# Differential attention, second layer: squares, lambda and the last transpositions at other places, one low weight part per head on VectorE

## The chip, the cores and the metric

One core of a Trainium2 chip (trn2) runs the program. TensorE (PE) multiplies and transposes. VectorE (DVE), ScalarE (ACT) and GpSimd (POOL) work element by element. SyncE (SP) issues the DMAs. The metric is the device time of one execution in microseconds.

## The reference

The model has two layers over 512 latent tokens and 256 context tokens of width 1024. The first layer has windowed and dense attention and is not touched. The second is differential attention with eight heads, and only it matters here:

```
hx = rms(x, w) * (1 + scale) + shift              # x: 512 x 1024;  hc the same from ctx: 256 x 1024
q, k, v = split([hc; hx] @ w_in)                  # eight heads, two q and two k of 64 each, v of 128
q, k = rope(rms(q)), rope(rms(k))                 # only the latent tokens are rotated
lam = exp(sum(lq1*lk1)) - exp(sum(lq2*lk2)) + lam_init
a = softmax(q0 k0^T / 8) - lam * softmax(q1 k1^T / 8)
o = rms(a @ v, subln) * (1 - lam_init)
x = x + gate * (o @ w_out);  then a feed-forward layer
```

## The kernel before

All large products are made in two parts: an operand is split into a high part (rounded, a cast on ScalarE) and a low part (what is left, a subtraction on VectorE or GpSimd), and hi·hi, lo·hi and hi·lo are summed in PSUM. The tokens lie in six tiles of 128: 0 to 3 are latent, 4 and 5 context.

The program is written as Python that calls the engines. TensorE's order is the order of writing. For the other engines a scheduler in the framework takes, by its own estimates, the next instruction that is ready; `behind(name)` keeps an instruction from being issued before the last one that was noted under this name in `turn`, and `tc.high_priority` lifts one. So a piece that is written elsewhere, or on another engine, moves neighbours too.

The second layer's attention goes like this.

- **Last normalizations** (`last_norm0`, `norm_steps`). For the latent tiles 1 to 3, ScalarE squares a row block of x and sums it (`nss`), GpSimd forms the inverse root (`rs_n`) and scales x (`nh`), TensorE transposes `nh` (`npt`), VectorE and ScalarE apply scale and shift and split the result into `hT` high and low. This is written between the first head's products (`inps`): context tiles 4 and 5, then tile 0, then tiles 1 to 3 together.
- **Projection** (`Proj1.sums`, `finish`). Per head and tile TensorE sums 1024 x 384 (context 256) products, with weight units of 256 rows: `wir` is loaded by DMA, `wih` is its cast, `wil` the subtraction (`weight1`, line 377). A head has four units, u = 0 to 3. Then ScalarE copies `inps` to `qkv`, VectorE and GpSimd rotate and normalize, and the casts `qd` and `kd` with their low parts go out. With `hold` these last are kept back, and written behind the copy of the next tile. TensorE transposes them later (`qpt`, `kpt`, from the list `late`), and ScalarE copies them to `qt` and `kT`.
- **Attention** (`attend1`). Each step is one tile of one head, 32 in all. TensorE makes two score tiles (`sc`), VectorE their maxima (`mx`), ScalarE exponentials with sums (`e`), VectorE combines them with lambda (`rt`, `e`), TensorE transposes (`ppt`), ScalarE copies four and VectorE two of the six pieces (`PT`), TensorE multiplies with V (`av`), ScalarE scales and squares (`o`), GpSimd forms `rs_o`, VectorE scales by it. Projection of the next head is written in three parts between the stages (`step`).
- **Tail.** In the last steps no projection is left, and the output projection (`opt`, `ops`, class `OutProj`) is written between the stages instead. `part(0)` is its first term, `oproj.operand` the transposition of `o` and its split.

All of this shares PSUM: two banks for transpositions (`tr_tile`, in turn), two for sums (`acc_tile`), and two pairs for scores (`sc`), of which the pairs hold tiles 0 to 3 of the first head before the first scores.

The line

```
                new_head([weight1(h, u, wh, nc.vector if h == 1 and u == 3 else nc.gpsimd) for u in range(4)])
```

sets the engine of each `wil` of heads 1 to 7: all on GpSimd but one.

Of the kernel before, what the change touches and what calls it, by code (L numbers as in the profile page):

```python
# [11 lines left out]
F32 = mybir.dt.float32  # L12
# [51 lines left out]
def backbone(es: ExitStack, tc: tile.TileContext, x, c, ctx, c_ctx, mod_w, mod_b, norm_mix_w, norm_ffn_w,  # L64
# [91 lines left out]
    def rsqrt(ss, n, inv, tag):  # L156

        r = small.tile([P, n], F32, name="rs_" + tag, tag="rs_" + tag)
        nc.gpsimd.tensor_scalar(r, ss, inv, EPS, ALU.mult, ALU.add)
        nc.gpsimd.tensor_tensor(r, r, neghalf[:, :n], ALU.pow)  # L160
        return r
# [164 lines left out]
    def tile_T(j, t):  # L326
        return cols_T(j, t * P, (t + 1) * P)

    def norm_steps(t, xt, l, f, pool, tags=(("nh", 2), ("nhc", 2)), room=None, bank=tr_tile, to=None, pool_scale=False):

        i = 0 if t < NTX else 1
        h, hc = room or (pool.tile([P, KT, P], F32, name=name, tag=tag, bufs=n)
                         for name, (tag, n) in zip(("nh", "nhc"), tags))
        halves = hc if isinstance(hc, list) else [hc[:, 0:4], hc[:, 4:8]]
        ss = small.tile([P, 1], F32, name="nss", tag="nss")
        xt = xt.rearrange("p (k c) -> p k c", c=P)
        turn["square"] = nc.scalar.activation(h, xt, AF.Square, accum_out=ss)
        r = rsqrt(ss, 1, 1.0 / D, "n")  # L340
        if pool_scale:
            turn["pool_scale"] = nc.gpsimd.tensor_scalar(h, xt, r, 1.0, ALU.mult, ALU.mult)
        else:
            turn[f"scaled{t}"] = nc.scalar.activation(h, xt, AF.Copy, scale=r)
        yield
        for g in range(2):
            pt = bank("npt", [P, 4, P])
            for k in range(4):
                turn["npt"] = nc.tensor.transpose(pt[:, k, :], h[:, 4 * g + k, :], ident)  # L349
            ks = slice(4 * g, 4 * g + 4)  # L350
            for k in range(4):
                kk = 4 * g + k
                sc, sh = aff[l][:, f, kk, i:i + 1], modc[l][:, 3 * f, kk, i:i + 1]
                if g:
                    nc.scalar.activation(halves[g][:, k], pt[:, k, :], AF.Identity, bias=sh, scale=sc)
                else:
                    nc.vector.tensor_scalar(halves[g][:, k], pt[:, k, :], sc, sh, ALU.mult, ALU.add)
            hi, lo = (to(j, g) if to else tile_T(j, t)[:, ks] for j in range(2))
            turn["hi"] = nc.scalar.copy(hi, halves[g])
            (nc.gpsimd if g and not pool_scale else nc.vector).tensor_sub(lo, halves[g], f32(hi))  # L360
# [1160 lines left out]
    if True:  # L1521
# [50 lines left out]
        def early_weight(u):  # L1572
            def room(shape, name):
# [5 lines left out]
        hooks = {(1, 0): [open_ctx], (1, 3): [finish_norm(4)], (1, 5): [finish_norm(5)], (1, 7): [finish_norm(0)],  # L1579
                 (1, 8): [small_loads], (1, 10): [lambda: ws1.append(head_tables(wt.pool, od_qn[0], od_kn[0], 2, 2))]}  # L1580
        hooks |= {(1, 12 + 2 * u): [early_weight(u)] for u in range(4)}
        way_out0(xs, hidm, out0.pool, places, raws, mod_hook1, hooks, done0)
    singles.close()
    p_sc = Pool("p_sc1", space=PSUM)
# [1 line left out]
    mods1.close()  # L1586
    wp = Pool("mw1", "right")
    wh = (whi.pool, wlo.pool)
    lqk, tabs = ws1[:2]
    del ws1[:2]  # L1590
    fp.close()
    at = Pool("mix1")
# [9 lines left out]
    def halves():  # L1602
        for h in range(1, 8):
            with behind(*("exp0",) * (h == 2)):
                new_head([weight1(h, u, wh, nc.vector if h == 1 and u == 3 else nc.gpsimd) for u in range(4)])
            for t in CTX_FIRST:
                ps = acc_tile("inps", one=0)
                state[h].sums(t, ps, range(4))
                yield t
                state[h].sums(t, ps, range(4, KT))  # L1610
                late.append((count + 5, state[h].finish(t, ps, count < 5)))
                yield t

    todo = halves()
# [11 lines left out]
    def last_norm0(t):  # L1626
        h, hc = (raw_tile([P, KT, P], "nhc") if t == 2 and i else keep.tile([P, KT, P], F32, name="nh", tag="xo", bufs=6)
                 for i in range(2))
        with tc.high_priority(300):
            for _ in norm_steps(t, xs[t], 1, 0, None, room=(h, hc), pool_scale=True):  # L1630
                pass

    if True:
        new_head(ws1)
        first = state[0]
        banks = {t: acc_tile("inps") for t in CTX_FIRST[:2]}
        for t in (0, 2):
            two = p_sc.pool.tile([P, 2, 512], F32, name="inps", tag="sc", bufs=2)
            banks.update({t + a: two[:, a, :] for a in range(2)})

        def ready(t):
            late.append((0, first.finish(t, banks[t], 0 < t < NTX)))

        for t in CTX_FIRST[:2]:
            first.sums(t, banks[t], range(KT))
# [16 lines left out]
        for i in range(6):  # L1662
            step()
            if i:
                turned()
        nlam = neg_lambda(lqk, cp)
        with behind("load"):
            subln = at.pool.tile([P, P], F32, name="subln")
            nc.sync.dma_start(subln, dram_rows(od_subln[0]))
            nc.gpsimd.tensor_scalar(subln, subln, 1.0 - LAM_INIT, 1.0, ALU.mult, ALU.mult)  # L1670
        xs0, xs1 = xs, [None] * NTX
        gate_mem(1, 5, 1)
        o_t = [keep.tile([P, D], F32, name=f"o{t}", tag="xo", bufs=6) for t in range(NTX)]
        xs = xs1
        attend = {}
# [8 lines left out]
        def transposed(i):  # L1684
            next(attend[i])
# [59 lines left out]
               *((nc.gpsimd, 4) if len(ws) in (3, 4, 6) else (nc.vector, 1)))  # L1745

        scores(last - 1)
        oproj.operand(0, ((0, 4),), acc1)
        transposed(last - 2)
        part(0)  # L1750
        while late:
            turned(True)
        values(last - 2)
        wp.close()
        wt.close()
        whi.close()
# [5 lines left out]
        opa = Pool("opa", "right")  # L1762
        oproj.gates(opa.pool)
        wo1()
        scores(last)
        transposed(last - 1)
        part(1, 2)
        values(last - 1)
        wo1()
        scores(last + 1)  # L1770
        oproj.operand(0, ((4, 7),), acc1)
# [192 lines left out]
```

## Time and profile before

| what | value |
|---|---|
| timed runs | 1684.29, 1685.66, 1688.02 us (median 1685.66) |
| profiled execution | 1689.65 us, of which the span of its instructions is 1687.9 |
| mean granted clock of TensorE | 0.994 |
| TensorE busy | 1629.1 us (97% of the span) |
| VectorE, ScalarE, GpSimd busy | 1141.2 (68%), 935.4 (55%), 715.6 us (42%) |
| the stretch touched | about 940 to 1340 us of the span |

Times in a trace are microseconds from the first instruction. Busy shares are averages over the whole span; what ends a wait is read from the place itself. TensorE is the busiest engine by far, so its idle time in the touched stretch is the first thing to look at.

### The profile page before, as it was taken

To read this page: it belongs to the slowest core of one execution; us is meant where nothing else is said; L and a number is where in the kernel's file an instruction comes from. 1 tells how busy PE (TensorE), PEld (TensorE's weight loads), DVE (VectorE), ACT (ScalarE), POOL (GpSimd) and SP (SyncE) were. 2 spreads that over 40 slices of the span, in tenths; PEclk is the share of its full clock that TensorE was granted. 3 is DMA by queue.
4 is the path that set the end of the run, shared out by engine and by line. 5 is a ranking of instruction groups with operands and counts; after the bars stand their busy time and mean duration, and the time that the engine had idled before them with its cause. 6 is when DMAs were issued, how large, how long until landed. Compare 5 with 4: busy or idle time off the path is not lost. (4 is left out here: it accounts for less than half of the span.)

```text
span 1687.9 us, 28522 instructions
## 1 busy us (share of the span) xinstructions
PE 1629.1 (97%) x10376; PEld 1467.2 (87%) x10376; DVE 1141.2 (68%) x1980; ACT 935.4 (55%) x2008; POOL 715.6 (42%) x872
## 2 busy tenths in 40 slices
PE   6989999899999999999999999999999999999998
PEld 3977787677999999998878899999988899999887
DVE  3765656554799987766767666666666598887433
ACT  5556565745556655544565456666666555555320
POOL 2665555621345564412413367776665342221000
PEclk8999999999999999999999999999999999999999
DMA  9221221421355555439956211111112333331431
GB/s 321 70 71 55 91 70 51 163 63 38 111 180 178 158 156 169 140 102 330 315 178 198 93 55 39 48 47 46 46 52 94 117 95 108 106 104 55 138 100 63
DMA packets 221692, 194.67 MB, mean 115 GB/s; under 512 B 20016, under 2 KB 206960, under 8 KB 221552
## 3 DMA queue, kind: packets, MB, share of 16 engines
q1 hardware_dynamic: 221200, 192.65, 37.1%
q8 instruction: 81, 1.33, 0.3%
q14 instruction: 59, 0.48, 0.1%
q10 hardware_dynamic: 352, 0.21, 0.0%
HBM read 179.94 MB, written 12.87 MB: 114 GB/s over the span
## 5 line engine op out<-in xcount | busy, mean ns | idle before, releaser
L925 ACT CAST wbh<-wr 128x512 fp32r<-128x512 f32 x170 | 104.8, 621 | 126.4 <-PE p L957 69.3
L957 PE MATMUL p<-hT,wbh 128*128 128x256 f32 (+1 forms) x752 | 154.0, 298 | 0.0
L471 PE MATMUL inps<-wih,hT 128*128 128x384 f32 x512 | 143.7, 343 | 2.9 <-ACT qkv L685 2.0
L935 POOL TENSOR_TENSOR wbl<-wr,wbh 128x512 fp32r<-128x512 f32 x43 | 59.2, 1377 | 174.5 <-ACT wbh L925 174.5
L957 PEld LDWEIGHTS p<-hT,wbh 128*128 128x128 f32 x752 | 122.1, 191 | 0.2
L935 DVE TENSOR_TENSOR wbl<-wr,wbh 128x512 fp32r<-128x512 f32 x127 | 107.8, 859 | 20.2 <-ACT wbh L925 16.0
L957 PE MATMUL p<-hT,wbl 128*128 128x256 f32 (+1 forms) x376 | 111.7, 297 | 0.0
L957 PE MATMUL p<-t,wbh 128*128 128x384 f32 (+1 forms) x480 | 110.8, 317 | 0.0
L231 POOL TENSOR_TENSOR modp<-modp 128x512 f32<-128x512 f32 x40 | 58.0, 1451 | 113.2 <-ACT modp L230 113.2
L610 POOL TENSOR_SCALAR Pt<-Pt,rc 128x256 f32<-128x256 f32 (+3 forms) x96 | 76.4, 809 | 66.7 <-DVE rc L607 57.9
L957 PE MATMUL p<-hTt,wbh 128*128 128x256 f32 (+1 forms) x480 | 100.8, 302 | 0.0
L911 POOL TENSOR_TENSOR wr<-wr 128x512 f32<-128x512 f32 x40 | 62.3, 1557 | 88.5 <-DVE ws L916 88.5
L471 PEld LDWEIGHTS inps<-wih,hT 128*128 128x128 f32 x512 | 93.4, 188 | 5.5 <-ACT qkv L685 3.0
L957 PE MATMUL p<-b,wbh 128*128 128x384 f32 x368 | 93.6, 335 | 1.3 <-DVE c L985 1.3
L925 ACT CAST wbh<-ws 128x512 fp32r<-128x512 f32 x120 | 69.5, 580 | 44.4 <-PE p L957 28.4
L224 DVE SCALAR_TENSOR_TENSOR ma<-modw,cols,ma 128x256 f32<-128x256 f32 x140 | 89.7, 641 | 2.4
L598 ACT ACTIVATE Pt<-sc,nm 128x256 f32<-128x256 f32 (+3 forms) x96 | 67.8, 709 | 36.6 <-DVE nm L594 17.4
L471 PE MATMUL inps<-wil,hT 128*128 128x384 f32 x256 | 85.8, 335 | 0.0
L935 DVE TENSOR_TENSOR wbl<-ws,wbh 128x512 fp32r<-128x512 f32 x120 | 81.7, 681 | 2.1 <-ACT wbh L925 2.0
L957 PEld LDWEIGHTS p<-t,wbh 128*128 128x128 f32 x480 | 82.8, 189 | 0.0
L957 PEld LDWEIGHTS p<-hTt,wbh 128*128 128x128 f32 x480 | 78.4, 191 | 3.0 <-ACT modp L230 2.1
L471 PE MATMUL inps<-wihi,hT 128*128 128x384 f32 x256 | 76.4, 355 | 2.0 <-DVE modc L279 1.8
(357 smaller groups left out, 5214.7 us busy)
## 6 DMA issues: line engine op xcount, KB each, us to landing
modw<-in_mod_w_dram SPq DMA_DIRECT2D x96, 512.0 KB, 4.8
wr<-in_ffn_w_in_dram SPq DMA_DIRECT2D x176, 256.0 KB, 3.0
wdr<-in_ffn_w_out_dram SPq DMA_DIRECT2D x66, 512.0 KB, 3.6
wir<-in_od_w_in_dram SPq DMA_DIRECT2D x96, 128.0 KB, 2.3
hidm<-hid SPq DMA_DIRECT2D x44, 192.0 KB, 3.0
hr<-hidm SPq DMA_DIRECT2D x22, 192.0 KB, 3.5
x<-in_x_dram SPq DMA_DIRECT2D x8, 512.0 KB, 8.8
wir<-in_ev_w_in_dram SPq DMA_DIRECT2D x16, 256.0 KB, 3.4
```

Of the source, the lines that this page charges most:

```text
L224: nc.vector.scalar_tensor_tensor(acc, w[:, k], scale[k], acc, ALU.mult, ALU.add)
L231: nc.gpsimd.tensor_add(pr[:, 0:2], pr[:, 0:2], pr[:, 2:4])
L471: nc.tensor.matmul(ps, hs[j][:, k, :], ws[k // 2][z][:, k % 2, c0:c1], start=(k, j, z) == (0, 0, 0), stop=(k, j, z) == (KT - 1, 1, 0))
L598: turn["exp"] = nc.scalar.activation(p[:, :n], s, AF.Exp, bias=nm[:, c1], accum_out=sm[:, c1])
L610: nc.gpsimd.tensor_scalar(p[:, :n], p[:, :n], rc[:, hh:hh + 1], 1.0, ALU.mult, ALU.mult)
L911: nc.gpsimd.tensor_sub(w, raw[f, "G1"], w)
L925: nc.scalar.copy(hi, w)
L935: (nc.gpsimd if name == "G2" else nc.vector).tensor_sub(lo, raw[need[n]], f32(hi))
L957: nc.tensor.matmul(ps, w[:, k, :], H[b][h][:, k, :], start=first and k == 0 and q == 0, stop=final and k == 3 and q == 2, skip_group_check ...
```

## The change

Seven edits, all in the second layer's attention and at its borders. The first is a new helper with its use: the squares and inverse roots of tiles 1 to 3 are called before the first head's products, and the unused squared rows go to the PSUM tile of tiles 2 and 3 instead of the tile that the scaled rows take.

```diff
+    def factor(xt, junk):
+        ss = small.tile([P, 1], F32, name="nss", tag="nss")
+        turn["square"] = nc.scalar.activation(junk, xt, AF.Square, accum_out=ss)
+        return rsqrt(ss, 1, 1.0 / D, "n")
...
-        ss = small.tile([P, 1], F32, name="nss", tag="nss")
         xt = xt.rearrange("p (k c) -> p k c", c=P)
-        turn["square"] = nc.scalar.activation(h, xt, AF.Square, accum_out=ss)
-        r = rsqrt(ss, 1, 1.0 / D, "n")
+        r = factor(xt, h) if r is None else r
...
+        hooks[1, 19] = [lambda: ws1.append(neg_lambda(ws1[0], cp))]
...
-                new_head([weight1(h, u, wh, nc.vector if h == 1 and u == 3 else nc.gpsimd) for u in range(4)])
+                new_head([weight1(h, u, wh, nc.vector if u == (3 if h == 1 else 1) else nc.gpsimd) for u in range(4)])
...
-                late.append((count + 5, state[h].finish(t, ps, count < 5)))
+                late.append((count + 5, state[h].finish(t, ps, count < 5 or count % 6 == 1)))
...
     if True:
+        gate_mem(1, 5, 1)
         new_head(ws1)
...
+        factors = {t: factor(xs[t], two.rearrange("p a b -> p (a b)")) for t in range(1, NTX)}
+
         def ready(t):
-            late.append((0, first.finish(t, banks[t], 0 < t < NTX)))
+            with behind("square"):
+                late.append((0, first.finish(t, banks[t], 0 < t < NTX)))
...
-        nlam = neg_lambda(lqk, cp)
...
-        gate_mem(1, 5, 1)
...
         scores(last - 1)
+        transposed(last - 2)
         oproj.operand(0, ((0, 4),), acc1)
-        transposed(last - 2)
+        turned(True)
+        values(last - 2)
         part(0)
+        scores(last)
+        transposed(last - 1)
         while late:
             turned(True)
-        values(last - 2)
+        values(last - 1)
...
-        scores(last)
-        transposed(last - 1)
         part(1, 2)
-        values(last - 1)
```

`neg_lambda` (two small products, an exponential with its table load, and two VectorE steps) is called 19 sums into the last feed-forward pass of the first layer; `gate_mem(1, 5, 1)`, which transposes the gate's row (`gps`), copies it (`grow`) and stores it by DMA, before the first head. Of heads 2 to 7 the low part of unit 1 goes from GpSimd to VectorE, six instructions of 128 x 768. Of each head one tile more is held back in `finish`. In the tail two things that stood behind the end of the list `late` are written ahead of its last entry. Apart from the six low parts no instruction changes its engine, and the count of TensorE's rows stays at 8120.

What this does to the order is shown at three places. The first is ScalarE while the last feed-forward sums of the first layer end and the first head begins; `x_4091`, `x_4250` and `x_4423` are the rows of tiles 1, 2 and 3. Before:

```order
L1022 CAST wdh<-wdr 128x1024
L339 ACTIVATE nh,nss<-x_4091 128x1024
L685 COPY qkv<-inps 128x256
L426 ACTIVATE sq<-qkv 128x128
L339 ACTIVATE nh,nss<-x_4250 128x1024
L339 ACTIVATE nh,nss<-x_4423 128x1024
L355 ACTIVATE nh<-npt,modc_107,aff_109 128x128 x4
```

and after:

```order
L1025 CAST wdh<-wdr 128x1024
L652 ACT_TABLE_LOAD
L652 ACTIVATE lex<-lps 128x2
L331 ACTIVATE inps,nss<-x_4091 128x1024
L331 ACTIVATE inps,nss<-x_4250 128x1024
L331 ACTIVATE inps,nss<-x_4423 128x1024
L688 COPY qkv<-inps 128x256
L429 ACTIVATE sq<-qkv 128x128
L358 ACTIVATE nh<-npt,modc_107,aff_109 128x128 x4
```

The three squares now stand one behind the other ahead of the first `qkv` copy, their output is in the tile `inps`, and the table load and the exponential of lambda are ahead of them.

The second is one head in the middle, first GpSimd before:

```order
L159 TENSOR_SCALAR rs_q<-qss 128x4
L377 TENSOR_TENSOR wil<-wir,wih 128x768
L160 TENSOR_TENSOR rs_q<-rs_q,neghalf 128x4
L377 TENSOR_TENSOR wil<-wir,wih 128x768
L159 TENSOR_SCALAR rs_o<-oss 128x1
L688 TENSOR_TENSOR qy<-qy,rs_q 128x256
L686 COPY vv<-qkv 128x128
L160 TENSOR_TENSOR rs_o<-rs_o,neghalf 128x1
L377 TENSOR_TENSOR wil<-wir,wih 128x768
```

and after:

```order
L159 TENSOR_SCALAR rs_q<-qss 128x4
L160 TENSOR_TENSOR rs_q<-rs_q,neghalf 128x4
L380 TENSOR_TENSOR wil<-wir,wih 128x768
L691 TENSOR_TENSOR qy<-qy,rs_q 128x256
L159 TENSOR_SCALAR rs_o<-oss 128x1
L689 COPY vv<-qkv 128x128
L160 TENSOR_TENSOR rs_o<-rs_o,neghalf 128x1
L703 TENSOR_TENSOR kd<-qy,kd 128x2x64
L380 TENSOR_TENSOR wil<-wir,wih 128x768
L159 TENSOR_SCALAR rs_q<-qss 128x4
```

then VectorE in the same stretch, before:

```order
L428 TENSOR_REDUCE qss<-sq 128x4
L751 SCALAR_TENSOR_TENSOR e<-e,rt 128x768
L438 TENSOR_TENSOR qy<-qkv,rt 128x256
L436 TENSOR_TENSOR qz<-qkv,rt 128x256
L740 TENSOR_REDUCE mx<-sc 128x1
L439 TENSOR_TENSOR qy<-qy,qz 128x256
L428 TENSOR_REDUCE qss<-sq 128x4
L740 TENSOR_REDUCE mx<-sc 128x1
L698 TENSOR_TENSOR qd<-qy,qd 128x256
L775 SCALAR_TENSOR_TENSOR o_10929<-o_10929,rs_o,subln 128x128
```

and after:

```order
L431 TENSOR_REDUCE qss<-sq 128x4
L754 SCALAR_TENSOR_TENSOR e<-e,rt 128x768
L380 TENSOR_TENSOR wil<-wir,wih 128x768
L441 TENSOR_TENSOR qy<-qkv,rt 128x256
L439 TENSOR_TENSOR qz<-qkv,rt 128x256
L743 TENSOR_REDUCE mx<-sc 128x1
L442 TENSOR_TENSOR qy<-qy,qz 128x256
L701 TENSOR_TENSOR qd<-qy,qd 128x256
L778 SCALAR_TENSOR_TENSOR o_10929<-o_10929,rs_o,subln 128x128
L743 TENSOR_REDUCE mx<-sc 128x1
```

One `wil` is on VectorE now, straight behind the combination `e`. On GpSimd the power step and `kd` stand ahead of a `wil` where they stood behind it, and on VectorE the scaling of `o` stands ahead of the second `mx` where it stood behind it; a `qd` subtraction that before stood behind both maxima is ahead of `e` in the tile before (not in these rows) and ahead of `o` here.

The third is TensorE in the tail, before:

```order
L822 MATMUL opt<-cst,o_10929 128x128 x4
L758 MATMUL ppt<-cst,e 128x128 x6
L831 MATMUL ops<-wo,hT_110 128x512
L832 MATMUL ops<-wo,hT_110 128x512
L833 MATMUL ops<-wo,hT_111 128x512
L716 MATMUL qpt<-identr,qd 128x128 x4
L722 MATMUL kpt<-identr,kd 128x128 x2
L716 MATMUL qpt<-identr,qd 128x128 x4
L722 MATMUL kpt<-identr,kd 128x128 x2
L768 MATMUL av<-vv,PT 128x128 x6
```

and after:

```order
L761 MATMUL ppt<-cst,e 128x128 x6
L825 MATMUL opt<-cst,o_10929 128x128 x4
L719 MATMUL qpt<-identr,qd 128x128 x4
L725 MATMUL kpt<-identr,kd 128x128 x2
L771 MATMUL av<-vv,PT 128x128 x6
L834 MATMUL ops<-wo,hT_110 128x512
L835 MATMUL ops<-wo,hT_110 128x512
L836 MATMUL ops<-wo,hT_111 128x512
```

`ppt` and `opt` change places, the first transpositions and a product with V stand ahead of the output projection's term (`ops`), and the second transpositions have left these rows: they come behind the eight score products and `ppt`.

## Rows read from the trace of the kernel before

**Rows 1.** Windows, one head: length, busy PE, PEld, DVE, ACT, POOL, granted clock, DMA.

```profile
1052.00:1091.00 39.00, 38.72 (x276) 37.48 (x275) 25.80 (x52) 25.67 (x68) 26.76 (x42) 1.00 0.15 42
```

**Rows 2.** Waits of TensorE, 940 to 1340 us: total, times, longest.

```profile
PE inps L471 <- ACT qkv L685: 2.0, 3, 1.0
...
PE ops L833 <- DVE hT L824: 1.7, 1, 1.7
...
PE inps L471 <- POOL wil L377: 1.7, 6, 0.3
...
PE qpt L716 <- ACT qd L697: 1.7, 1, 1.7
...
PE npt L349 <- POOL nh L342: 1.2, 2, 0.6
...
PE inps L471 <- DVE hT L360: 0.9, 1, 0.9
...
PE gps L293 <- ACT kT L723: 0.6, 1, 0.6
```

**Rows 3.** Timeline, start of the second layer: start, duration, instruction, [idle before].

```profile
949.01 1.06 ACT L339 ACTIVATE nh<-x 128x1024 f32<-128x1024 f32 x1 [7.01 <-DVE x L478]
...
951.18 1.14 POOL L342 TENSOR_SCALAR nh<-x,rs_n 128x1024 f32<-128x1024 f32 x1
...
953.73 0.69 DVE L478 TENSOR_TENSOR x<-x,dps 128x512 f32<-128x512 f32 x1
...
955.67 1.04 PE L349 MATMUL npt<-cst,nh 128*128 128x128 f32 x8
```

**Rows 4.** Timeline of VectorE and GpSimd in one head.

```profile
1048.73 0.43 DVE L438 TENSOR_TENSOR qy<-qkv,rt 128x256 f32<-128x256 f32 x1 [0.90 <-ACT qkv L685]
...
1054.67 1.85 POOL L377 TENSOR_TENSOR wil<-wir,wih 128x768 fp32r<-128x768 f32 x1
...
1055.71 1.10 DVE L438 TENSOR_TENSOR qy<-qkv,rt 128x256 f32<-128x256 f32 x1 [3.94 <-ACT qkv L685]
```

**Rows 5.** Timeline: VectorE's one low part (head 1), then three engines in one head.

```profile
978.95 0.96 DVE L377 TENSOR_TENSOR wil<-wir,wih 128x768 fp32r<-128x768 f32 x1 [1.24 <-ACT wih L376]
...
1050.76 1.01 DVE L751 SCALAR_TENSOR_TENSOR e<-e,rt 128x768 f32<-128x768 f32 x1
...
1053.69 1.02 POOL L160 TENSOR_TENSOR rs_q<-rs_q,neghalf 128x4 f32<-128x4 f32 x1
...
1056.94 0.68 POOL L688 TENSOR_TENSOR qy<-qy,rs_q 128x256 f32<-128x256 f32 x1
...
1057.22 0.83 ACT L376 CAST wih<-wir 128x768 fp32r<-128x768 f32 x1 [0.54 <-DMA wir<-in_od_w_in_dram]
...
1058.34 1.83 POOL L377 TENSOR_TENSOR wil<-wir,wih 128x768 fp32r<-128x768 f32 x1
...
1058.60 0.94 DVE L740 TENSOR_REDUCE mx<-sc 128x1 f32<-128x768 f32 x1
```

**Rows 6.** Timeline of GpSimd and TensorE in the tail.

```profile
1260.25 1.31 POOL L688 TENSOR_TENSOR qy<-qy,rs_q 128x256 f32<-128x256 f32 x1
...
1263.14 2.61 PE L768 MATMUL av<-vv,PT 128*128 128x128 f32 x12
...
1269.02 1.59 PE L768 MATMUL av<-vv,PT 128*128 128x128 f32 x12
...
1270.37 0.36 PE L735 MATMUL sc<-kT,qt 128*128 128x256 f32 x1
```

**Rows 7.** Timeline of TensorE in the first layer, a long wait.

```profile
199.67 0.66 PE L618 MATMUL ppt<-cst,Pt 128*128 128x128 f32 x4 [2.64 <-ACT qt L543]
```

**Rows 8.** Windows behind that wait, around another, and in the tail (as rows 1).

```profile
200.00:204.00 4.00, 4.00 (x20) 3.38 (x19) 2.73 (x7) 0.28 (x3) 1.58 (x2) 0.57 0.64 206
...
844.00:852.00 8.00, 6.55 (x28) 4.89 (x27) 5.14 (x7) 4.11 (x7) 2.65 (x2) 1.00 0.69 192
...
1262.00:1265.00 3.00, 2.94 (x15) 2.78 (x16) 0.42 (x1) 2.00 (x5) 0.52 (x2) 0.50 0.38 70
```

More of the change, by code (lines that the diff above doesn't have):

```diff
@@ L327, in tile_T, with norm_steps @@
         return cols_T(j, t * P, (t + 1) * P)
-    def norm_steps(t, xt, l, f, pool, tags=(("nh", 2), ("nhc", 2)), room=None, bank=tr_tile, to=None, pool_scale=False):
+    def factor(xt, junk):
+        ss = small.tile([P, 1], F32, name="nss", tag="nss")
+        turn["square"] = nc.scalar.activation(junk, xt, AF.Square, accum_out=ss)
+        return rsqrt(ss, 1, 1.0 / D, "n")
+    def norm_steps(t, xt, l, f, pool, tags=(("nh", 2), ("nhc", 2)), room=None, bank=tr_tile, to=None, pool_scale=False, r=None):
         i = 0 if t < NTX else 1
@@ L1588, in backbone @@
     wh = (whi.pool, wlo.pool)
-    lqk, tabs = ws1[:2]
+    tabs, nlam = ws1[1], ws1.pop()
     del ws1[:2]
@@ L1629, in last_norm0 @@
         with tc.high_priority(300):
-            for _ in norm_steps(t, xs[t], 1, 0, None, room=(h, hc), pool_scale=True):
+            for _ in norm_steps(t, xs[t], 1, 0, None, room=(h, hc), pool_scale=True, r=factors.get(t)):
                 pass
     if True:
+        gate_mem(1, 5, 1)
         new_head(ws1)
```

## Prediction

> **What bounds the kernel now.** I read the windows and the waits first, then the order in time of the four engines wherever the order of instructions changes. In a whole head of layer 1 the matmuls fill 38.72 of 39.00 us at the full clock [rows 1]. So an edit there pays only if it takes away a wait of TensorE. The waits of the touched stretch, 940 to 1340 us, are few [rows 2]. Those that the edits can reach are 2.0 us for copies of qkv (three, the longest 1.0), 1.7 for hT in the tail, 1.7 for the low weight part (six of 0.3, one per head), 1.7 for a qd cast in the tail, 1.2 for the scaled rows nh (two), 0.9 for hT of the last normalization, and 0.6 before the gate's transposition. They sum to 9.8 us, 0.6% of the run. Nearly no instruction is added, so what counts is which of these go, and which new ones come.
>
> **Early squares.** Before, ScalarE squares x1 at 949.01, and GpSimd has x1 scaled (nh) at 951.18 + 1.14 = 952.32, 3.31 us after the square began. TensorE transposes it at 955.67 with no wait [rows 3]. In the new order all three squares stand ahead of the next qkv copy, and they write their unused result into a PSUM tile of layer 1. Its bank last held feed-forward sums of x3. So the first square may not begin before the last addition to x3 has read them, 953.73 + 0.69 = 954.42, or a little later for the small gate copy now queued on VectorE ahead of that addition. The same 3.31 us then lead to 957.7 or a little more: TensorE is there at 955.67, and a wait of 2.2 appears where there was none. The squares of x2 and x3 follow at 1.06 each and are in time, so the two waits for nh (1.2) go. The 0.9 for hT stays, because the products that feed it come later by the rest. Net +1.0. Bounds: -2.1, if the squares did run early and all these waits went, and +1.1. So this edit would not do what its code says: the squares move ahead in the list, but the first one starts 5.4 us later.
>
> **Lambda and gate.** Two small products, the table load, the exponential and the gate's transposition leave the place where the scores begin. There TensorE stood 0.6 us [rows 2]. At the new place, beside feed-forward matmuls, ScalarE and VectorE have nothing to do, so there they cost TensorE their own short products and no wait; I count 0.3 more for leaving a place where they ran singly between waits, an estimate of half the stall. The exponentials then start about 0.9 earlier, and the longest wait for qkv, 1.0, which comes behind two of them, shrinks by about 0.4. The next wait for qkv near there, some 0.3, goes since the held casts stand behind the copy. Sum -1.6. Bounds -2.0 and -0.6.
>
> **Low weight part on VectorE.** VectorE and GpSimd hold each other up. VectorE's product of qkv and a table takes 0.43 alone. Started beside GpSimd's subtraction, which ran from 1054.67 to 1056.52, it took 1.10 and ended 0.29 after that one [rows 4]. The moved subtraction reads two tiles from SBUF like that product, and is 0.96 long [rows 5]. If nothing were held up, the third unit's low part would come 1.8 earlier and the six waits would go, -1.7; if the two engines exclude each other, the term changes sign, as follows.
>
> The Trainium skill states it as a rule ("SBUF — State Buffer", section "Who interferes with whom"): a VectorE instruction with two SBUF inputs contends with a GpSimd one that reads SBUF, and whichever is second fully blocks. The trace agrees with its 1.10 for 0.43; by that rule the term is the +2.4 below, without it -1.7.
>
> Follow one head [rows 5]. Before, the third unit's low part runs from 1058.34 to 1060.17, and TensorE waits 0.3 for it. After: a qd subtraction of some 0.4 now stands before the combination e on VectorE, so e ends not at 1051.77 but at 1052.2. The new subtraction follows at once, to 1053.1. GpSimd's power step, now ahead of its own first subtraction, gets through at about 1053.0 and takes 1.02, to 1054.0; the subtraction 1.83, to 1055.8; the scaling of qy 0.68, to 1056.5. ScalarE's qd and kd casts, now ahead of a square and of the third unit's cast, need that qy. They and the square take some 0.9 and the cast 0.83, to 1058.2. So the third unit's low part starts at about 1058.3, as before. The 1.8 taken off GpSimd is spent on the later e, on the blocking, and on steps that were put ahead. And there is a new piece. VectorE's scaling of o now stands ahead of the second maximum, which before was at 1058.60 beside GpSimd's subtraction and, reading PSUM, was not held up. If the scaling meets that subtraction it waits until 1060.1, the maximum is 1.8 late, and so is the copy of the last P pieces behind it, for which TensorE's product with V waits. I take +0.4 a head, 0.2 for the low part and 0.2 for that copy: 6 x 0.4 = +2.4. Bounds: -0.3 a head (-1.7) if nothing is blocked, +0.6 a head (+3.6) if every meeting falls badly. The value lies nearer the upper end, as the row of 1.10 is of just this meeting.
>
> **Held casts.** One tile per head has its qd and kd casts behind the next copy. In the middle heads TensorE waits for no copy, so they give nothing beyond what is counted above. The third wait for qkv, 0.6 at 1247, goes too, but brings the products with V nearer to the P copies that ScalarE makes; I take nothing. Bounds -0.6 and +0.3.
>
> **Tail.** Before, TensorE stands 1.7 for hT and 1.7 for qd [rows 2]. Then its clock is half, and the product with V takes 2.61 where the next one takes 1.59 [rows 6]: 1.0 lost, and 0.6 more on the transpositions just ahead of it, in proportion. After, the projection's operand, tile 2's transpositions and a product with V come sooner, each with a wait of its own (I count 2.0 in all, mostly for a copy that stands behind a maximum and a sum on VectorE). The next scores are done at about 1263.2, their P transpositions at 1263.8. Then tile 3's transposition needs a bank that ScalarE frees with its next P copy, and that copy is late. Its chain starts where GpSimd ends qy, 1260.25 + 1.31 = 1261.56; two casts, two steps on o, two on GpSimd, o's scaling, a maximum of 0.94, an exponential and the copy follow, some 5 us, to 1266.6. TensorE waits 2.8. The work up to the next scores brings them to 1270.1 at full clock, 1270.37 before: -0.3, and +1.3 if the clock falls as it did.
>
> **The clock.** Which of its two levels (1.2 and 2.4 GHz) TensorE is granted after a wait is read in three places [rows 7, 8]. After 2.64 idle the mean is 0.57 over four microseconds, so half for most of them. After the two waits of 1.7 it is 0.50. After 1.45 idle (8.00 less 6.55) it stays 1.00. The tail's 2.8 is like the first, so I take the half clock there, +1.3. The early 2.2 lies between; I take it without, and with it 1.6 comes on top.
>
> **Sum.** +1.0 - 1.6 + 2.4 + 1.3 = +3.1 us. The profiled execution took 1689.65, 1.75 more than its span and 4.0 more than the median of the timed runs, 1685.66; the same difference is added to that median: 1688.8. About 0.2%, 3.4 us, is what a measurement of this kernel can tell from no change.
>
> **Rivals.** The first is the other side, the squares do run early and the two engines rarely meet: -2.1 - 1.6 - 1.7 - 0.3 = -5.7, 1680.0. It is decided by the first square's start: at 949 the waits for nh go, past 952.4 a wait appears. The dependence speaks against it; chance 0.10. The second: the early wait comes, but the third unit's low part is really 1.8 earlier: +1.0 - 1.6 - 1.7 + 1.3 = -1.0, 1684.7. For it speaks that VectorE is idle for 3.94 in that place, against it the 1.10; chance 0.16. The third: the clock holds in the tail, +1.0 - 1.6 + 2.4 - 0.3 = +1.5, 1687.2; chance 0.22, since the half clock of before came after two waits. The fourth: the clock falls at the early wait as well, +3.1 + 1.6 = +4.7, 1690.4; chance 0.20. The forecast has 0.32.
>
> **Numbers.** Slower by over 0.2% are the fourth rival and the upper part of the forecast's own case (3.6 for 2.4 in the heads): 0.33. Faster are the first rival and a little of the second: 0.13. The rest, 0.54, is within 0.2%. The range leaves out the first rival and what lies beyond the fourth with its heads at the upper bound: 1681.5 to 1692. The likeliest case by itself reaches from 1685, if half of the heads are spared, to 1690.4.
>
> **What would show it.** The first square at 954.4 or later and a TensorE wait for nh of about 2 us near 957; no wait at 995; six waits for the low part still there, 0.3 to 0.7 each, and new ones for a P copy on VectorE; VectorE's scaling of o at 1.5 or more beside GpSimd's subtraction; one wait of 2 to 3 us near 1265 with half clock behind it. The prediction is wrong if the six waits are gone, or if the first square starts at 949.

## The result and the profile after

Timed side by side on one chip, the changed kernel takes 1692.38 us (median of 11 runs, 1690.12 to 1695.73) and the kernel before 1688.02 (11 runs, 1684.29 to 1693.95). The medians differ by 4.4 us. The ratio on record is 1.0022, 95% interval 1.0011 to 1.0032, which is 3.7 us slower, and that is the number compared below. The forecast was +3.1. The number 1692.38 itself lies just above the range, because before, in this comparison, is 2.4 above the 1685.66 to which the forecast was added. The profiled execution took 1694.6 us, its span 1692.8, with a mean granted clock of 0.992.

The waits of TensorE in the changed stretch (total, times, longest), which answer to [rows 2]:

```profile
PE inps L474 <- POOL wil L380: 3.0, 6, 0.5
PE av L771 <- ACT PT L766: 2.7, 6, 1.2
PE npt L352 <- POOL nh L345: 1.9, 1, 1.9
PE qpt L719 <- ACT PT L766: 1.4, 1, 1.4
PE kpt L725 <- DVE PT L764: 1.2, 1, 1.2
...
PE inps L474 <- DVE hT L363: 0.6, 1, 0.6
...
PE inps L474 <- ACT qkv L688: 0.4, 1, 0.4
```

The waits for qkv and for the gate shrank or went, as forecast. The six for the low weight part grew from 1.7 to 3.0. One wait of 1.9 for nh stands in place of two of 0.6, and the 0.9 for hT is 0.6. And the product with V now waits for P copies of ScalarE. The windows of one head and of the tail (columns as rows 1):

```profile
1052.00:1091.00 39.00, 38.34 (x270) 36.65 (x269) 26.68 (x50) 24.40 (x67) 25.98 (x41) 1.00 0.14 42
...
1265.00:1268.00 3.00, 3.00 (x14) 2.81 (x14) 1.71 (x2) 1.26 (x5) 1.25 (x2) 0.50 0.00 0
```

Against [rows 1], TensorE idles 0.38 us more in these 39 us, and 270 of its matmuls fall into them for 276. The order in time, at the start of layer 1, in one head and in the tail:

```profile
955.11 0.67 DVE L481 TENSOR_TENSOR x<-x,dps 128x512 f32<-128x512 f32 x1
...
955.81 1.03 ACT L331 ACTIVATE inps<-x 128x1024 f32<-128x1024 f32 x1 [9.71 <-DVE x L481]
...
959.15 1.09 PE L352 MATMUL npt<-cst,nh 128*128 128x128 f32 x8 [1.91 <-POOL nh L345]
...
1052.69 0.95 DVE L380 TENSOR_TENSOR wil<-wir,wih 128x768 fp32r<-128x768 f32 x1
...
1052.92 1.61 POOL L160 TENSOR_TENSOR rs_q<-rs_q,neghalf 128x4 f32<-128x4 f32 x1
...
1058.88 2.01 POOL L380 TENSOR_TENSOR wil<-wir,wih 128x768 fp32r<-128x768 f32 x1
...
1059.13 1.91 DVE L778 SCALAR_TENSOR_TENSOR o<-o,rs_o,subln 128x128 f32<-128x128 f32 x1
...
1060.94 0.39 PE L474 MATMUL inps<-wil,hTc 128*128 128x256 f32 x1 [0.49 <-POOL wil L380]
1060.96 0.94 DVE L743 TENSOR_REDUCE mx<-sc 128x1 f32<-128x768 f32 x1
...
1061.64 1.69 PE L771 MATMUL av<-vv,PT 128*128 128x128 f32 x12
...
1062.16 0.41 DVE L764 COPY PT<-ppt 128x256 f32<-128x256 f32 x1
...
1062.32 0.20 POOL L159 TENSOR_SCALAR rs_q<-qss 128x4 f32<-128x4 f32 x1 [1.43 <-DVE qss L431]
...
1069.20 0.30 ACT L702 CAST kd<-qy 128x128 fp32r<-128x128 f32 x1 [0.65 <-POOL qy L691]
1069.40 0.90 ACT L745 ACTIVATE e<-sc,mx 128x768 f32<-128x768 f32 x1
...
1070.49 0.57 ACT L766 COPY PT<-ppt 128x512 f32<-128x512 f32 x1
...
1071.12 1.05 PE L771 MATMUL av<-vv,PT 128*128 128x128 f32 x7 [0.16 <-ACT PT L766]
...
1263.96 0.34 PE L725 MATMUL kpt<-identr,kd 128*128 128x128 f32 x2 [1.25 <-DVE PT L764]
1264.46 2.81 PE L771 MATMUL av<-vv,PT 128*128 128x128 f32 x12 [0.17 <-DVE hT L827]
...
1271.84 0.54 PE L719 MATMUL qpt<-identr,qd 128*128 128x128 f32 x4 [1.40 <-ACT PT L766]
```

The first square begins at 955.81, 0.03 after the last addition to x3 has ended: it waits for the bank, as forecast. In the head the power step takes 1.61 beside VectorE's low part, for 1.02 [rows 5], and the scaling of o 1.91 beside GpSimd's. The second maximum stands behind that scaling, and VectorE's P copy and qss behind the maximum. Two things come of it. The product with V takes 1.69 for its twelve matmuls, where in before the same product, not shown so far, took 1.50:

```profile
1060.92 1.50 PE L768 MATMUL av<-vv,PT 128*128 128x128 f32 x12
```

The last four of the twelve read the two pieces that VectorE copies. Eight start 0.11 apart; the ninth starts 0.20 behind the eighth, at 1062.62, 0.05 after the copy has ended at 1062.57. And GpSimd stands idle for 1.43 until qss. Its later steps shift with that: ScalarE's kd cast waits 0.65 for GpSimd's qy; the exponential and the P copy stand behind it, and TensorE behind the copy.

Total times hide where this comes from: executions of one kernel (ten or more of them) differ by 4 to 11 us, and in single traces the same instruction at 940 us, ahead of every edit, stands 5.8 us earlier to 0.8 later than in the profile of before. So each trace is read by stages. For each TensorE instruction I took its start less that of the same instruction in the profile of before (the median over the next 6 us); the table says how much this shift grows in a stage, in us, over before's times 940 to 1012 (start), 1012 to 1240 (heads) and 1240 to 1330 (tail). From 1330 to the end the shift changes by 0.01 at most, in all kernels but e4; outside the touched stages the traces differ ahead of 940, and hardly behind 1330.

```
kernel              edits                      start  heads   tail   ratio (95%)
after               all seven                  -1.15  +5.12  +0.20   1.0022 (1.0011 to 1.0032)
e1_wil_only         5: low part                -0.26  +5.40  +1.26   1.0046 (1.0034 to 1.0059)
e2_hold_only        6: held casts              -0.46  +2.95  +1.23   1.0019 (1.0009 to 1.0029)
e3_no_wil           all but 5                  -1.08  +2.60  -0.85   1.0013 (1.0003 to 1.0022)
e4_reduction        none; unused maxima        +0.22  +0.12  +0.66   0.9982 (0.9973 to 0.9990)
e5_psum_squares     1, 2: squares              +0.40  -0.17  +0.47   1.0016 (1.0006 to 1.0026)
e6_sbuf_squares     squares, output in SBUF    -2.49  -0.24  +0.41   0.9991 (0.9981 to 1.0001)
e7_lambda_gate      3, 4: lambda, gate         -0.49  -0.29  +1.17   1.0002 (0.9992 to 1.0012)
e8_squares_lambda   e6 and e7                  -2.43  -0.77  +0.25   0.9981 (0.9968 to 0.9995)
e9_control          none                       -0.02  -0.16  +0.91   0.9999 (0.9989 to 1.0009)
e10_tail_only       7: tail                    +0.67  +0.16  -0.11   0.9990 (0.9981 to 0.9999)
e11_two_inputs      none; unused, two operands -0.03  +1.17  +0.60   1.0010 (1.0001 to 1.0019)
e12_all_good        e8 and 7                   -2.94  -0.45  -0.01   0.9970 (0.9958 to 0.9981)
```

Where a stage is untouched, its shift lies between -0.26 and +0.67 in the start, -0.77 and +0.16 in the heads, and +0.25 and +1.26 in the tail. The start of e2 isn't counted as untouched: its -0.46 is one wait for qkv, 0.33 at 1009 in before, which the held casts take away there. Only what leaves these bands is called an effect.

### The profile page after: what moved, and what is told of

The parts are those of the page before. It is cut to its first block, busy times and chain, and to the rows that moved or that the text cites. A ratio compares the mean times of both kernels' runs of the same rounds, so it can differ in the third digit from the quotient of the medians.

```text
span 1692.8 us, 28506 instructions
## 1 busy us (share of the span) xinstructions
PE 1632.3 (96%) x10376; PEld 1468.2 (87%) x10376; DVE 1157.3 (68%) x1986; ACT 933.0 (55%) x2008; POOL 707.8 (42%) x866
## 4 chain that ended last, share of the span: by engine, by line
PE 43%; DVE 5%; ACT 3%; POOL 2%; DMA 1%; issue 1%; SPq 0%; DVEq 0%; POOLq 0%; ACTq 0%
PE p L960 12%; PE inps L474 7%; PE dps L1057 3%; PE dps L1058 3%; PE dps L1059 3%; PE dps L1104 2%; PE dps L1103 2%; PE dps L1105 2%; PE av L771 2%; PE pz L960 2%; ACT e L745 1%; DMA wdr<-in_ffn_w_out_dram 1%; DVE mx L743 1%; DVE o L778 1%; PE sc L738 1%
## 5 line engine op out<-in xcount | busy, mean ns | idle before, releaser
L745 ACT ACTIVATE e<-sc,mx 128x768 f32<-128x768 f32 x64 | 57.7, 902 | 45.4 <-DVE mx L743 45.4
```

The source lines that it names most:

```text
L745: turn["exp"] = nc.scalar.activation(e, S[a], AF.Exp, bias=mx[:, a:a + 1], accum_out=sm[:, a:a + 1])
```

## The experiments

**The low part alone**, before with the fifth edit.

```diff
-  nc.vector if h == 1 and u == 3 else nc.gpsimd
+  nc.vector if u == (3 if h == 1 else 1) else nc.gpsimd
```

> The kernel before with edit 5 alone: unit 1's low part of heads 2 to 7 on VectorE. Theory 1 (VectorE and GpSimd hold each other up, and that is what the middle heads lose): slower than before by 2 to 4 us (ratio 1.001 to 1.0025), TensorE still waits in each of heads 2 to 7 for the third unit's low part, 0.3 us or more, and GpSimd's power step beside the moved subtraction takes about 1.6 instead of 1.0. Theory 2 (the held casts make the loss): no loss, and the six waits of 0.3 go, 1.7 faster. Theory 3 (VectorE's added time, not the port): slower, like the run with a reduction added.

Measured: 1694.93 for 1687.26, heads +5.40, beyond the 2 to 4 expected. It costs more alone than in the full change. The timeline of one head:

```profile
1057.19 3.81 POOL L377 TENSOR_TENSOR wil<-wir,wih 128x768 fp32r<-128x768 f32 x2 [0.95 <-ACT wih L376]
...
1066.70 0.30 ACT L699 CAST kd<-qy 128x128 fp32r<-128x128 f32 x1 [0.72 <-POOL qy L688]
1066.91 0.37 ACT L685 COPY qkv<-inps 128x256 f32<-128x256 f32 x1
...
1067.33 0.44 PE L471 MATMUL inps<-wih,hT 128*128 128x384 f32 x1 [0.59 <-ACT qkv L685]
```

GpSimd makes two of its three remaining subtractions back to back, 3.81 us, so its power steps and qy come late, a kd cast on ScalarE waits for them, and the copy that frees a bank waits behind that cast. How much of the 5.4 is the two engines' exclusion and how much this order, no run separates.

**The held casts alone**, before with the sixth edit.

```diff
-  late.append((count + 5, state[h].finish(t, ps, count < 5)))
+  late.append((count + 5, state[h].finish(t, ps, count < 5 or count % 6 == 1)))
```

> The kernel before with edit 6 alone: one more tile per head with its qd and kd casts behind the next qkv copy. Theory 1: as before within 0.1%, since TensorE waits for no copy there. Theory 2 (the casts, now queued on GpSimd, ScalarE and VectorE ahead of the third unit's cast and low part, make that part late): slower by 2 to 4 us, with the six waits for the low part at 0.6 or more. A third reading has both edits costing about 3 us alone, and not 6 together, as each delays the same low part.

Measured: 1690.72 for 1687.26, heads +2.95; the six waits for the low part are 5.1 in all (1.7 before), the longest 1.1. ScalarE and GpSimd in one head, first in before, not shown so far:

```profile
1048.22 0.48 ACT L685 COPY qkv<-inps 128x384 f32<-128x384 f32 x1 [0.82 <-PE inps L471]
...
1049.95 0.44 ACT L426 ACTIVATE sq<-qkv 128x256 f32<-128x256 f32 x1
...
1051.90 1.84 POOL L377 TENSOR_TENSOR wil<-wir,wih 128x768 fp32r<-128x768 f32 x1
```

and with the held casts:

```profile
1045.91 0.48 ACT L685 COPY qkv<-inps 128x384 f32<-128x384 f32 x1 [0.82 <-PE inps L471]
1046.29 0.41 ACT L697 CAST qd<-qy 128x256 fp32r<-128x256 f32 x1
1046.59 0.30 ACT L699 CAST kd<-qy 128x128 fp32r<-128x128 f32 x1
1046.79 0.91 ACT L742 ACTIVATE e<-sc,mx 128x768 f32<-128x768 f32 x1
...
1048.15 0.43 ACT L426 ACTIVATE sq<-qkv 128x256 f32<-128x256 f32 x1
...
1050.09 1.84 POOL L377 TENSOR_TENSOR wil<-wir,wih 128x768 fp32r<-128x768 f32 x1
...
1058.42 0.39 PE L471 MATMUL inps<-wil,hTc 128*128 128x256 f32 x1 [0.79 <-POOL wil L377]
```

From the copy of qkv to its square it is 1.73 us before and 2.24 with the casts between, to GpSimd's first subtraction 3.68 and 4.18. Both are 0.5 later, in every head about so, and 6 x 0.5 = 3.0 is the 2.95 of the table. The casts stand behind one copy, but ahead of an exponential, a P copy and a square.

**All but the low part**: the changed kernel with the fifth edit undone.

```diff
-  nc.vector if u == (3 if h == 1 else 1) else nc.gpsimd
+  nc.vector if h == 1 and u == 3 else nc.gpsimd
```

> The changed kernel without edit 5 (the low parts back on GpSimd), all else kept. Theory 1: the loss of the heads goes, about 4 us faster than the changed kernel, and at or below before. Theory 2: it stays slower than before by 2 to 4 us. If both edits cost, as in the third reading, it lies 1 to 2 us below the changed kernel and 2 to 3 above before.

Measured: 1689.04 for 1687.26, heads +2.60, as with the held casts alone. So the low part adds 5.12 - 2.60 = 2.5 to a kernel that has the held casts. The six waits for the low part are longer here than in the changed kernel, 4.7 in all for 3.0: the moved part does shorten them, and loses more elsewhere. The tail is 0.85 shorter, at full clock throughout, also behind a wait of 1.25 that ends at 1254.97:

```profile
1255.00:1258.00 3.00, 2.83 (x20) 2.55 (x21) 2.52 (x5) 2.06 (x8) 2.15 (x3) 1.00 0.00 0
```

**An unused maximum on VectorE.** Before, with a maximum over unit 1's high part behind e in heads 2 to 7: as long as the moved low part, with one operand.

```diff
...
+  if h > 1:
+      top = small.tile([P, 1], F32, name="top", tag="top")
+      nc.vector.tensor_reduce(top, f32(ws_h[1][0]).rearrange("p a b -> p (a b)"), AX.X, ALU.max)
```

> The kernel before with one step added: in heads 2 to 7 VectorE also takes the maximum over unit 1's high part (128 x 768, one tile read, about 0.95 us, unused result), at the place where the moved subtraction stands; GpSimd keeps all its low parts. Theory 1: no change (within 0.1%), as a step that reads one tile holds nobody up and VectorE is idle for 3.9 us there. Theory 3 (any 0.95 us more on VectorE at that place delays what follows): slower by 2 us or more.

Measured: heads +0.12. The maximum took 0.95 us and GpSimd's subtraction beside it 1.84, as ever. An added 0.95 us of VectorE costs nothing here. The whole kernel was 0.18% faster, in parts that the edit does not touch (below).

**Two operands on VectorE.** Before, with six unused steps per head in the same place, each a maximum of two operands from SBUF.

```diff
...
+  if h > 1:
+      whl = ws_h[1][0].rearrange("p a b -> p (a b)")
+      for c in range(6):
+          nc.vector.tensor_tensor(spare, f32(whl[:, c * P:(c + 1) * P]), f32(whl[:, c * P:(c + 1) * P]), ALU.max)
```

> Before with six unused VectorE steps of 128x128 per head, straight behind the combination e of heads 2 to 7, each a maximum of two operands from SBUF (both the high part of unit 1); nothing else changes its place. They take about as long together as the moved low part, and as the reduction of the earlier run, which had one operand and left the heads unchanged (+0.1). If two operands from SBUF on VectorE hold up GpSimd's subtraction, which begins beside them, that one ends some 0.6 to 1 later in each head, the third unit's low part too, and TensorE waits for it by as much more: heads +2 to +5, waits for the low part 0.6 to 1.2 each for 0.3. If VectorE's time is what counts, or the steps only wait themselves in VectorE's idle stretch, heads 0 to +0.3.

Measured: heads +1.17, between the two. The view of this tile in one head (count: shortest, median and longest in ns), and the timeline:

```profile
L1609 DVE TENSOR_TENSOR spare<-wih x6: 284/292/1879, 1046.8 to 1050.0; 128x128 bf16<-128x128 f32 x6
```

```profile
1046.80 5.06 DVE L1609 TENSOR_TENSOR spare<-wih 128x128 bf16<-128x128 f32 x6
1047.01 1.84 POOL L377 TENSOR_TENSOR wil<-wir,wih 128x768 fp32r<-128x768 f32 x1
1048.80 1.07 POOL L160 TENSOR_TENSOR rs_q<-rs_q,neghalf 128x4 f32<-128x4 f32 x1
1049.85 1.85 POOL L377 TENSOR_TENSOR wil<-wir,wih 128x768 fp32r<-128x768 f32 x1
1051.79 0.45 POOL L159 TENSOR_SCALAR rs_o<-oss 128x1 f32<-128x1 f32 x1
```

Steps of 0.29 alone take 5.06 together: two of them met a subtraction of GpSimd and took up to 1.88. The subtractions kept their 1.84 and 1.85. Here VectorE is the one that is held up, and it loses much of the 3.9 us in which it was idle [rows 4]. The +1.17 comes in steps of about 0.25 at the third low part: GpSimd's small steps took 1.07 and 0.45 here, for 1.02 and 0.25 in before, so the third subtraction is as much later. By the Trainium skill ("SBUF — State Buffer", section "Who interferes with whom") a VectorE instruction with two SBUF inputs contends with a GpSimd instruction that reads SBUF, and a reduction never does on trn2. Both runs agree: 1.88 for 0.29, and 0.95 for the maximum.

**Early squares, output in PSUM**: before with edits 1 and 2.

```diff
...
+  factors = {t: factor(xs[t], two.rearrange("p a b -> p (a b)")) for t in range(1, NTX)}
...
```

> The kernel before with edits 1 and 2 alone, the unused squares in the PSUM tile as in the change. Theory 1 (the tile keeps the first square back until the last addition to x3): the first square starts 5 to 6 us later than before, a wait of about 2 us for nh stands ahead of the first transposition, the two later waits for nh go, and TensorE is about 1 us later at the end of this stage; the run 0 to 0.1% slower. Rival (the squares run early): the first starts where it did, the waits for nh go, 1 to 2 us earlier at the end of the stage.

Measured: ratio 1.0016, a little more than expected; start +0.40, which the band can't tell from nothing; up to 977 us, behind the normalizations, it is +0.68. The first square in the timeline:

```profile
949.00 1.03 ACT L331 ACTIVATE inps<-x 128x1024 f32<-128x1024 f32 x1 [12.45 <-DVE x L481]
```

This trace stands 5.46 earlier than before's at 940, so that is 954.46 in before's times, right where the forecast had it (954.42 or a little later).

**Early squares, output in SBUF**: the same, but the unused rows go to tiles that nothing else holds then.

```diff
...
+  room1 = [keep.tile([P, KT, P], F32, name="nh", tag="xo", bufs=6) for i in range(2)]
+  factors = {t: factor(xs[t], room1[t > 1].rearrange("p k c -> p (k c)")) for t in range(1, NTX)}
```

> The same as the run with PSUM squares, but the unused squares go to SBUF, into the two tiles that tile 1 takes later anyway (its scaled rows and their second half), allocated a little earlier. Theory 1 (only the PSUM tile kept the squares back): the first square starts right after the addition to x1, no wait for nh is left in this stage, and TensorE is 1 to 2 us earlier at its end than before, so 2 to 3 us earlier than with PSUM squares. Rival (something else is late there): no change against the PSUM run.

Measured: start -2.49; the waits for nh are gone.

```profile
945.45 1.06 ACT L331 ACTIVATE nh<-x 128x1024 f32<-128x1024 f32 x1 [7.01 <-DVE x L481]
```

With the shift of 3.56 this is 949.01, the start of before [rows 3]. So the first rival, squares that really run early, hangs on the output tile alone.

**Lambda and gate**: before with edits 3 and 4.

```diff
+  hooks[1, 19] = [lambda: ws1.append(neg_lambda(ws1[0], cp))]
...
+  gate_mem(1, 5, 1)
   new_head(ws1)
...
```

> The kernel before with edits 3 and 4 alone: lambda and the gate's transposition at their earlier places. Theory 1: no wait of TensorE at the first scores, the next wait for qkv shorter by some 0.4; TensorE is 1.0 to 1.9 us earlier from the first head on than before, after about 0.5 lost where the two small products stand among the feed-forward sums; 0.05 to 0.1% faster. Rival (the products only move their cost, with it the wait): no change.

Measured: 1686.94 for 1687.08, start -0.49, less than expected. TensorE's wait for qkv up to 1000 us:

```profile
PE inps L471 <- ACT qkv L685: 0.4, 1, 0.4
```

The gate's wait of 0.6 is gone and that of 1.0 for qkv went to 0.4, but of these 1.2 us only 0.5 arrives. The instructions are paid for at their new place (the shift grows by 0.5 at lambda's products and 0.1 at the gate's transposition), and the next wait for qkv, at 1003, is 0.73 where it was 0.33.

**Squares in SBUF with lambda and gate**: both edits of the two runs above.

```diff
+  hooks[1, 19] = [lambda: ws1.append(neg_lambda(ws1[0], cp))]
...
+  gate_mem(1, 5, 1)
   new_head(ws1)
...
+  factors = {t: factor(xs[t], room1[t > 1].rearrange("p k c -> p (k c)")) for t in range(1, NTX)}
```

> SBUF squares and edits 3 and 4 together, without the low parts on VectorE, the held casts and the new tail. By theory 1 the two gains add up: TensorE 2.5 to 4 us earlier from the first head on than before, the middle heads as before, and the run 0.15 to 0.25% faster than before. If they share a wait, 1 to 2 us.

Measured: 1683.71 for 1687.08, ratio 0.9981, start -2.43, just short of the 2.5 to 4 expected and no more than the squares alone: the two gains don't add up. This kernel is faster than both before and the changed one.

**The same kernel again**, before with one comment line more.

```diff
+    # the same kernel
```

> The kernel before with one comment line more and no other difference. It shows what two builds of the same instructions differ by. If the spread between builds is what moved the reduction kernel (0.9982 with nothing changed in the stages around its edit), this one may lie anywhere within 0.2% of before, and its shift at 940 us against the profile of before is somewhere between 0 and -5.8. If a build of the same instructions always takes the same time, the ratio is 1.0000 within 0.0008, and the shift at 940 comes from the one profiled execution of before.

Measured: 1688.02 for 1687.84, ratio 0.9999. But in its trace the tail is 0.91 longer than in the profile of before. The windows of TensorE's half clock there, first in before:

```profile
1261.00:1264.00 3.00, 1.95 (x10) 1.78 (x11) 0.52 (x2) 1.68 (x6) 1.02 (x2) 0.65 0.22 20
1264.00:1267.00 3.00, 3.00 (x19) 2.78 (x19) 0.51 (x1) 1.63 (x4) 2.07 (x3) 0.78 0.86 333
```

and in this kernel:

```profile
1261.00:1264.00 3.00, 3.00 (x15) 2.83 (x16) 0.39 (x1) 1.94 (x4) 0.59 (x2) 0.50 0.32 67
1264.00:1267.00 3.00, 3.00 (x14) 2.67 (x14) 0.72 (x1) 0.77 (x3) 2.85 (x5) 0.57 1.03 418
```

Behind the same two waits (1.71 and 1.65 us, for 1.72 and 1.66) the clock is half for 6.8 us, where it was 3.4 in before's. Of the ten traces with the old tail eight have 6.8 us of half clock there, and only before and e8 have 3.4. The tail that the forecast started from was a short one.

**The tail alone**: before with the seventh edit.

```diff
...
+  scores(last)
+  transposed(last - 1)
...
```

> Before with the seventh edit alone: the last transpositions written one tile on. By the prediction's term the tail (1250 to 1330 us) gets 1.3 longer if TensorE's clock falls to half behind the wait near 1265, and 0.3 shorter if it stays full. By the runs so far, 0.4 longer (the changed kernel, half clock seen for 3 us) or 0.6 shorter (without the moved low part, full clock). Heads unchanged, 0 within 0.3. Time: within 0.1% of the control kernel.

Measured: 1685.62 for 1687.84, ratio 0.9990; tail -0.11, with half clock for 3.4 us (0.59 is the mean of the window):

```profile
1255.00:1258.00 3.00, 2.52 (x12) 2.39 (x13) 2.80 (x6) 1.74 (x5) 2.07 (x4) 0.59 0.00 0
```

**What was good, together**: squares in SBUF, lambda, gate and the new tail, edits 5 and 6 left out.

```diff
+  hooks[1, 19] = [lambda: ws1.append(neg_lambda(ws1[0], cp))]
...
+  factors = {t: factor(xs[t], room1[t > 1].rearrange("p k c -> p (k c)")) for t in range(1, NTX)}
...
+  scores(last)
+  transposed(last - 1)
...
```

> Before with the squares early into tiles of SBUF that are free, lambda and gate early, and the new tail; without the moved low part and the held casts. Against the kernel with the same squares and lambda but the old tail (0.9981): 0.6 less if the tail runs at full clock, 0.4 to 1.3 more if it falls to half. So 0.9977 to 0.9989; start of layer 1 -2.4, heads 0.

Measured: 1682.53 (5 runs) for 1687.84, ratio 0.9970, 5 us faster than before; a little better than expected. Start -2.94, heads -0.45, tail -0.01.

## Why the prediction was right, and where not

The direction and about the size hold: +3.1 forecast, +3.7 measured, just beyond what can be told from no change. But that the sum came so near is luck: the heads lost over twice what was forecast, the start gained more, and the tail lost less.

**Early squares** (forecast +1.0; rival one). The mechanism is right: the first square behind the last addition to x3, and a wait of 1.91 for nh. The size was less: for the two edits alone +0.68 behind the normalizations and +0.40 at the end of the stage. The wait for hT, which was to stay at 0.9, is 0.6. With the output in SBUF the wait for nh is gone, and the term is -2.5.

**Lambda and gate** (forecast -1.6). Alone the two edits give -0.5. But the forecast counted on the held casts for the last wait for qkv, and rightly: with them alone its 0.33 is gone, and without them it grows. Step by step in the changed kernel, the shift grows by 0.65 at the new places, and falls by 1.14 at the first scores and by 0.62 and 0.42 at the two waits for qkv. That is -1.5, near the forecast.

**Low weight part** (forecast +2.4; rival two). The exclusion is shown: the power step at 1.61, the scaling of o at 1.91, six waits of 0.5, and the 1.88 of the unused steps. Rival two falls. The forecast followed one head with the held casts in it, so its +2.4 stands against the +5.12 of the heads, beyond its upper bound of 3.6. Both waits that it counted came, at their size. In one head the shift grows by 0.22 at the wait for the low part (0.2 forecast), and by 0.19 inside the product with V that waits for VectorE's late P copy (0.2 forecast; so in five of the six heads, with no wait listed). What it left out is a third wait, +0.44 at the next product with V, which waits for ScalarE's P copy (in four heads; in the last it is 1.06). In the trace that copy goes back to the same blocked scaling of o (no run tried it by itself): the maximum and qss are late behind it, GpSimd's next row and its qy behind qss, and ScalarE's kd cast, exponential and copy behind qy. Beside the held casts the edit costs +2.5, alone +5.4; alone another order leaves two subtractions of GpSimd back to back.

**Held casts** (forecast 0). This step failed: "In the middle heads TensorE waits for no copy, so they give nothing beyond what is counted above." They give nothing, but without the low part they cost 2.6 to 2.95. The two casts stand ahead of ScalarE's exponential, and through the square they make GpSimd's whole row of subtractions 0.5 late, in a head in which TensorE waits for the third of these. It was asked which wait they end, and not who stands behind them. The two edits don't add up: 5.40 and 2.95 alone, 5.12 together.

**Tail and clock** (forecast +1.3; rival three). This failed too, in the other direction. The first waits came as forecast, 0.44, 1.25 and 0.17 for 2.0 in all. But half clock followed these already, for 3.4 us from 1264.6, and the wait for tile 3's bank is 1.40 and not 2.8, with full clock behind it. Half clock also costs less there than the 1.6 that was taken, since part of it comes off a wait that would come anyway: at full clock, with the low part undone, that wait is 1.94. Three of the four kernels with the new tail have 3.4 us of half clock (0.50, 0.59 and 0.61 in windows of 3 us) and shifts of -0.11 to +0.20; the fourth has full clock and -0.85. With the old tail, 6.8 us of half clock go with +0.41 to +1.26, and 3.4 us with 0 (before's own profile) and +0.25. So at equal half clock the two tails take about the same time. In the mean the new one is 1.0 shorter (-0.2 for +0.8), as the half clock was shorter in its few traces; what sets its length stays open. The whole times agree with a gain: 0.9990 for the tail alone, and 0.9970 for 0.9981 with the squares and lambda.

**The early clock** (rival four). It stayed at 1.00 behind the wait of 1.91, as taken.

In sum, against kernels with the same stage untouched (means: start +0.12, heads -0.23, tail +0.77): -1.27 + 5.35 - 0.57 = +3.5, for 3.7 measured. By stage the forecast was -0.6 + 2.4 + 1.3. What was left out in the heads, 2.9, and what was charged too much elsewhere, 2.5, make up for each other.

## What to carry to other kernels

Of an instruction that is moved on an engine that seems idle enough, ask who stands behind it there, and follow that one to the engine with no slack; two casts of 0.7 us together ahead of an exponential cost as much as the weight part that was moved for a purpose. An early instruction is early only if its output tile is free, and an unused output is best put where nothing else was. Below 0.3% a total time says little of an edit: rebuild the kernel before without a change, and compare stages of the traces with that, not with a single profile.

## What the runs showed of the hardware

A wait listed as 0.16 for a P copy moved all that follows by 0.44, and a shift of 0.19 came where no wait is listed, between the eighth and the ninth of twelve matmuls of one row. The starts of the same instructions in two traces show such waits.

The same waits in the tail are followed by half clock of 3.4 us in some executions and 6.8 in others, and with the new tail once by none. The place in the first layer that the prediction read as full clock behind 1.45 us of idle has 2.18 in the changed kernel's execution, in two waits of 1.12 and 1.06, and 0.57 as the mean clock from 848 to 852 us. What decides it stays open.

With the unused maxima, matmuls of one line and shape were closer together in the last feed-forward layer, which the edit does not touch. Before and that kernel, by line and shape, 50 us each (count, busy us, mean ns):

```profile
L957 PE MATMUL p<-hT,wbl 128*128 128x256 f32 x60 | 17.0, 283 | 0.0
```

```profile
L957 PE MATMUL p<-hT,wbl 128*128 128x256 f32 x60 | 16.7, 279 | 0.0
```

The granted clock is 1.00 in both. Over that stage the shift falls by 3.4 us, in no other kernel by more than 0.01, and this kernel was faster by 0.18%, 3.0 us; the cause was not tried.
